# A two-layer decoder step: transposing a layer's outputs at the spill instead of at the load, and preparing a head's weights one head ahead

## The chip, the cores and the metric

The kernel runs on one NeuronCore of a Trainium2 chip. The metric is the time of one execution on the device, in microseconds (us). The core has a matrix engine (TensorE, PE in the profile, its weight loads PEld), three engines for elementwise work (VectorE = DVE, ScalarE = ACT, GpSimd = POOL), and SyncE (SP), which here only issues DMAs. Sixteen DMA engines move data between DRAM and the on-chip SBUF; matrix products land in PSUM. Each engine runs its own instructions in order and waits on semaphores for the others. So does SP: an issue that waits holds up every issue behind it.

## The reference

One inference step of a two-layer decoder, for a prompt of 2048 tokens and 8 samples of 4 tokens, with 1024 features:

```python
# layer 0: gated linear attention, 4 heads, key width 128, value width 512
proj = rmsnorm(h, norm_g) @ w_in              # q, k, v, gate, g_low
log_a = log_sigmoid(g_low @ w_gate2 + b_gate) / 16
o, state = gla_recurrence(q * 128**-0.5, k, v, log_a, state0)
h = h + (rmsnorm(o, out_norm_g) * silu(gate)) @ w_out
# keys and values shared by the next layer, from rmsnorm(h)
k, v = rope(rmsnorm(u @ w_k, k_norm)), u @ w_v
# layer 1: attention over a window of 128 positions, 32 query heads, 4 key heads
q, gate = split(rmsnorm(h, norm_g) @ w_in)
o = attend(rope(rmsnorm(q, q_norm_g)), k, v, sinks)
h = h + (o * silu(gate)) @ w_out
```

Inputs, weights and outputs are fp32. The outputs are both groups' results, the recurrent states of layer 0 and the last keys and values.

## The kernel before

**Numbers.** Each fp32 operand of a product is split into two fp16 halves, hi and lo, and the product is three fp16 matmuls (`PASSES`, L277). `split` (L184) makes the halves: ACT copies to fp16, and DVE or POOL subtracts. A weight is converted in steps of 128 x 512 elements (`Unit.convert`, L206): SP loads it raw into `wraw`, ACT scales and rounds it, DVE computes the remainder. Two ways lead from there:

- `load` (L229) converts straight into a buffer `W`, from which TensorE reads. There are 12 such buffers, each for 1024 columns, so for two steps.
- `prepare` (L234) converts into one of two `pst` buffers, and POOL issues a DMA that writes the halves to DRAM (`pre`, L242). Later `fetch` (L246) has SP load all of a unit into a `W`. Prepared steps are emitted with a lower priority (`behind`, L168).

**Layer 0** runs over 4 heads and, within a head, over 4 blocks (j = 0 to 3) of 512 tokens: 16 blocks (the loop at L926). A block computes q and k (48 matmuls of 512 columns), v and the gate for 4 chunks of 128 tokens (192), the block's scores by levels of halving with decays (`level_steps`, L487), and for each chunk the state update, the output and its norm (`chunk_steps`, L553). `weave` and `mix` (L145, L162) interleave lists of steps. Each block computes q, k and levels of the next one. The update of the states reads `ke`, the decayed keys, which SP transposes by DMA once per block (L545). In the first block of a head the 8 samples' states pass through (`sparts`), each by way of a `pst` buffer (L763).

At the end of a chunk `spill_og` (L607) splits its 128 x 512 outputs into halves in `ogT` (two buffers), ACT for hi and POOL for lo, and SP writes them to DRAM, `ogd[c]` (L610), tokens on the partitions.

The head's own weights come at two places. The q and k weights of the next head are loaded in its third block (L968 to L972). The v and gate weights are loaded and converted, 16 steps of `load`, in its last block: v at L953, when the old v weights are done with, the gate at L958.

The weights of layer 1 and combinations of its output weights are prepared in advance: a list `prep` of 144 steps (L866, L887), 8 rotary tables first, then 72 weight steps, then 64 steps for the combinations. `some(n)` (L868) takes the next n. In blocks from the third on, L966 takes `PR[j]` of them for each of three chunks, with `PR = (1, 4, 2, 0)`; so 3, 12, 6 and 0 a block, 63 in layer 0 in all. The last two blocks load the output weights of layer 0 instead.

**The output projection of layer 0** (`a_out`, L1034) runs over 16 chunks of 128 tokens, each 96 matmuls of 512 columns. `load` fetches a chunk's outputs with four transposing DMAs of 256 KB (L1041), so that features are on the partitions; it is called one chunk ahead (L1101, L1105). `fin` adds the residual, norms it and transposes the result by DMA into `uT` for layer 1. The first four chunks are woven into the end of layer 0's last block, with `few = 2` prepared steps in each of the chunks 1 to 3 (L1097 to L1102); the chunks 4 to 13 take `each = 7` (L1098, L1106), and the rest, 5, go to the end (L1491).

**Layer 1** runs 64 blocks in an order of TensorE that is written out (L1501), and then its output projection. Its own spill (`spill_halves`, L612) already transposes from SBUF to SBUF before it writes.

The order of instructions on each engine is otherwise made by a scheduler at build time, from the program's order, priorities and a simulated timeline.

Of the kernel before, what the change touches and what calls it, by code (L numbers as in the profile page):

```python
# [19 lines left out]
P = 128  # L20
# [32 lines left out]
SMC = 3  # L53
NV = 5
KL = 5
QL = 9
PR = (1, 4, 2, 0)

# [16 lines left out]
def _body(tc, nc, cp, sb, ps, dr, i, o):  # L75
# [12 lines left out]
    def C(tag, shape, dt):  # L88
        return cp.tile(shape, dt, tag=tag, name=tag)
# [28 lines left out]
    make_identity(nc, idh)  # L118
    mhalf = C("mhalf", [P, 16], F32)
    pool.memset(mhalf, -0.5)  # L120
# [16 lines left out]
    rtd = dr.tile([P, NCH, 4, HD], F32, tag="rtd", name="rtd")  # L137
    ogd = [dr.tile([P, 2, BW], F16, tag=f"ogd{c}", name=f"ogd{c}") for c in range(NCH)]
    ogd2 = [dr.tile([P, 2, 2, 8, P], F16, tag=f"oge{c}", name=f"oge{c}") for c in range(NCH)]
# [467 lines left out]
    def spill_og(og, dst, h, eng):  # L607
        ot = T("ogT", [P, 2, 512], F16, 2)
        split((ot[:, 0], ot[:, 1]), og, eng=eng)
        nc.sync.dma_start(dst[:, :, h * 512 : (h + 1) * 512], ot)  # L610

# [256 lines left out]
    def some(n=2):  # L868
        out = prep[:n]
        del prep[:n]  # L870
        return out
# [51 lines left out]
    samp = None  # L923
    sparts = []

    for n, (h, j) in enumerate(blocks):  # L926
# [7 lines left out]
        elif n == 1:  # L934
            side = u_steps(3) + [us_step]
        lv = nxt.level_steps() if nxt else []
        last = j == NBL - 1
        late = j == 0 and h > 0
# [11 lines left out]
        if last:  # L950
            ch = [cur.chunk_steps(c) for c in range(3)]
            weave([f for c in range(1, 4) for f in cur.vg_steps(c, (0,))], ch[0] + lv[:3] + ch[1][:3] + lv[3:5] + ch[2][:3])
            run(hw[h + 1].v.steps() if h + 1 < AH else wo.steps()[4:])  # L953
            for c in range(1, 4):
                weave(cur.vg_steps(c, (1,)), (ch[c - 1][3:] if c > 1 else []) + lv[3 + c * 2 : 5 + c * 2])
            for f in ch[2][3:]:
                f()
            run(hw[h + 1].g.steps() if h + 1 < AH else wo1.steps()[8:])  # L958
        else:
            for c in range(3):  # L960
                if n == len(blocks) - 2:
                    if c == 0:
                        wo_aside()
                    more = (wo1.steps()[:8] + wo.steps()[:4])[c * 4 : c * 4 + 4]
                else:
                    more = side[c * 2 : c * 2 + 2] if n < 2 else some(PR[j])  # L966
                weave(cur.vg_steps(c + 1, (0, 1) if n else (1,)), mix(cur.chunk_steps(c) + lv[(0,3,6)[c]:(3,6,8)[c]], sparts[(0,3,7)[c]:(3,7,99)[c]]) + more)
                if j == NBL - 2 and h + 1 < AH and c == 0:  # L968
                    hw[h + 1] = head_weights(h + 1)
                    for u in hw[h + 1].qk:  # L970
                        for f in u.steps():
                            f()  # L972
            sparts = []
# [60 lines left out]
    def a_out(c):  # L1034
# [3 lines left out]
        def load():  # L1038
            for q in range(4):
                ot.append(box_o["first"][:, q] if c == 0 else T(("sg", "v")[c % 2], [P, 8, P], F16, 4))  # L1040
                nc.sync.dma_start(ot[q], ogd[c][:, q % 2, q // 2 * D : q // 2 * D + D], transpose=True)  # L1041

# [52 lines left out]
    lead = 4  # L1095
    few = 2
    each = (len(prep) - 3 * few) // (tail - lead + 1) + 1  # L1097
# [207 lines left out]
    class SampleB:  # L1305
# [22 lines left out]
        def steps(self):  # L1328
# [141 lines left out]
            def att_3(tq):  # L1470
                Pc, VC, Vn = bx["Pc"], bx["VC"], bx["Vn"]
                pO = PT("kv", [P, GRP // 2, 4, TS])
                for b4 in range(4):
                    b = tq * 4 + b4
                    for pr in range(2):
# [4 lines left out]
                        for n, (a, z) in enumerate(PASSES):  # L1480
                            mm(out, Vn[:, z, :], rr(Pc[:, 1, a, b4]), start=False, stop=n == 2)
                of = T("skn2", [P, GRP // 2, 16], F32, 1)
                tk = slice(tq * 16, tq * 16 + 16)
# [342 lines left out]
```

## Time and profile before

| | us |
|---|---|
| median of 3 runs | 2831.7 |
| fastest, slowest | 2829.96, 2833.98 |
| the profiled execution | 2836.73 |
| its span, first to last instruction | 2834.9 |
| mean granted TensorE clock in it | 0.986 |

The stages of the profiled execution follow from the profile's matmuls: head 0 of layer 0 to about 345 us, heads 1 to 3 about 273 us each, the start of the output projection from about 1170, its steady part from 1245 to 1520, layer 1 to 2550 and its output projection to the end. A window's row in the profile gives the length of a stretch, the busy time of PE, PEld, DVE, ACT and POOL with their instruction counts, the granted TensorE clock as a share of full speed, the mean share of the DMA engines that were busy, and GB/s. A row of waits gives the total, the number of times and the longest. A row of a line gives count, shortest/median/longest duration in ns, and when the first and the last of them started. "SPq" is SP's issue of a DMA: its start and how long it took to issue. Matmuls are pipelined: one of 512 columns is shown with 379 ns, but 24 of them follow each other in 5.18 us.

### The profile page before, as it was taken

What the parts mean: (1) busy time and instruction counts of PE and PEld (TensorE: products, weight loads), DVE (VectorE), ACT (ScalarE), POOL (GpSimd) and SP (SyncE); (2) the same over time, 40 slices, a digit from 0 to 9 for tenths busy, and PEclk for the clock granted to TensorE, in tenths of its full rate; (3) what the DMA queues carried; (4) which work ended last, traced back from release to release, by engine and by line L of the source; (5) the groups of instructions that cost most, each with busy time, mean ns of one, the idle gap of its engine ahead of it and who ended that gap; (6) DMA issues with size and microseconds to landing.
All of it is one profiled execution on the core that took longest, in us unless ns stands there. A gap on an engine that the chain in (4) does not pass through costs nothing.

```text
span 2834.9 us, 51733 instructions
## 1 busy us (share of the span) xinstructions
PE 2716.0 (96%) x19258; PEld 1388.1 (49%) x19258; DVE 1699.3 (60%) x3470; ACT 1392.5 (49%) x3245; POOL 1145.7 (40%) x1600
## 2 busy tenths in 40 slices
PE   6899998999899999999899999999999999989999
PEld 4444544544454445444344555555555555544444
DVE  5665666566657655335422665677777777777653
ACT  6554655455546553433322555566666666651110
POOL 2352244224323421125503686566567567530000
PEclk9999999999999999999999999999999999999999
DMA  8351334134313533799987678978888899996431
GB/s 210 87 128 35 101 105 148 34 86 138 116 38 86 167 90 81 184 214 260 258 183 190 129 146 152 226 133 157 187 149 151 155 189 185 177 220 201 154 99 57
DMA packets 801029, 411.69 MB, mean 145 GB/s; under 512 B 644352, under 2 KB 717896, under 8 KB 800744
## 3 DMA queue, kind: packets, MB, share of 16 engines
q1 hardware_dynamic: 787816, 372.66, 57.5%
q0 software_dynamic: 10880, 35.66, 3.7%
q8 instruction: 150, 2.46, 0.4%
q14 instruction: 103, 0.84, 0.1%
q10 hardware_dynamic: 2080, 0.07, 0.0%
HBM read 161.97 MB, written 107.54 MB: 95 GB/s over the span
## 4 chain that ended last, share of the span: by engine, by line
PE 60%; DMA 9%; ACT 9%; DVE 8%; issue 6%; POOL 5%; SPq 1%; ACTq 0%; POOLq 0%; DVEq 0%
PE pj L101 35%; PE o L101 11%; PE tr L101 9%; PE kv L101 3%; ACT o L1261 2%; DVE v L192 2%; DMA pre<-pst 1%; PE lev L101 1%; ACT v L191 1%; DMA wraw<-in_a_w_in_dram 1%; DVE o L1256 1%; POOL ogT L189 1%; DMA pst<-v 1%; DMA uT<-ogT 1%; DVE lev L1256 1%
## 5 line engine op out<-in xcount | busy, mean ns | idle before, releaser
L101 PE MATMUL pj<-W,uT 128*128 128x512 f16 x5088 | 1198.8, 381 | 6.2 <-ACT sg L481 3.6
L101 PEld LDWEIGHTS <-uT 128*128 128x128 f16 x6976 | 650.5, 98 | 711.3 <-issue 36.7
L101 PE MATMUL tr<-W,uT 128*128 128x512 f16 x1536 | 365.6, 379 | 0.0
L180 POOL TENSOR_SCALAR rs_m<-ss 128x1 f32<-128x1 f32 (+3 forms) x186 | 40.0, 215 | 537.0 <-DVE ss L1158 186.2
L101 PEld LDWEIGHTS <-X 128*128 128x128 f16 x2744 | 185.1, 98 | 141.5 <-issue 15.8
L1261 ACT ACTIVATE o<-o,mx 128x256 f32<-128x256 f32 (+1 forms) x384 | 168.7, 439 | 165.9 <-DVE mx L1256 162.0
L101 PE MATMUL pj<-uT,W 128*128 128x512 f16 (+1 forms) x912 | 190.2, 358 | 26.1 <-DMA uT<-ogT 22.6
L1256 DVE CUSTOM_DVE_ANT_0 o<-o,madd,nsink 128x256 f32<-128x256 f32 (+1 forms) x384 | 183.8, 479 | 38.6 <-PE o L101 34.2
L192 DVE SCALAR_TENSOR_TENSOR v<-o,v 128x512 f16<-128x512 f32 (+1 forms) x192 | 129.0, 672 | 104.4 <-ACT v L191 102.2
L181 POOL TENSOR_TENSOR rs_r<-rs_m,mhalf 128x1 f32<-128x1 f32 (+3 forms) x182 | 185.0, 1016 | 13.4
L514 POOL TENSOR_TENSOR KQ<-KQ,bt 128x256 f32<-128x256 f32 x112 | 97.7, 873 | 229.1 <-DVE X L189 229.1
L101 PEld LDWEIGHTS <-W 128*128 128x128 f16 x2448 | 129.6, 99 | 114.2 <-issue 23.2
L101 PEld LDWEIGHTS <-v 128*128 128x128 f16 x976 | 95.3, 98 | 116.4 <-issue 4.4
L189 POOL TENSOR_TENSOR ogT<-og,ogT 128x512 f16<-128x512 f32 x68 | 82.2, 1208 | 123.8 <-ACT ogT L188 123.8
L101 PEld LDWEIGHTS <-sg 128*128 128x128 f16 x800 | 78.4, 99 | 106.3 <-DMA sg<-ogd 11.7
L188 ACT ACTIVATE X<-KQ 128x512 f16<-128x512 f32 x128 | 84.6, 661 | 74.2 <-PE lev L101 46.8
L101 PE MATMUL o<-gl,X 128*128 128x256 f16 (+1 forms) x768 | 113.9, 271 | 3.1 <-DMA X<-qe 1.7
L189 DVE TENSOR_TENSOR X<-KQ,X 128x512 f16<-128x512 f32 x128 | 98.5, 770 | 28.4 <-ACT X L188 27.4
L191 ACT ACTIVATE v<-o 128x512 f16<-128x512 f32 (+1 forms) x192 | 111.1, 579 | 3.6
L242 POOL DMA_DIRECT2D pre<-pst x72 | 50.4, 702 | 142.2 <-DVE pst L192 111.7
L1261 ACT ACTIVATE lev<-lev,mx 128x256 f32<-128x256 f32 (+1 forms) x128 | 56.5, 441 | 103.6 <-DVE mx L1256 101.5
L101 PE MATMUL pj<-W,v 128*128 128x512 f16 x448 | 104.4, 379 | 0.4 <-DMA v<-ogd 0.4
(437 smaller groups left out, 4848.0 us busy)
## 6 DMA issues: line engine op xcount, KB each, us to landing
pre<-pst POOLq DMA_DIRECT2D x72, 256.0 KB, 3.4
W<-pre SPq DMA_DIRECT2D x36, 512.0 KB
ogd<-ogT SPq DMA_DIRECT2D x68, 256.0 KB
wraw<-in_a_w_in_dram SPq DMA_DIRECT2D x64, 256.0 KB
wraw<-in_b_w_in_dram SPq DMA_DIRECT2D x64, 256.0 KB
oge<-og SPq DMA_DIRECT2D x64, 256.0 KB
wraw<-in_a_w_out_dram SPq DMA_DIRECT2D x32, 256.0 KB
X<-in_x_prompt_dram SPq DMA_DIRECT2D x32, 256.0 KB
```

Of the source, the lines that this page charges most:

```text
L101: return order(nc.tensor.matmul(*a, **k))
L180: pool.tensor_scalar(m[:n, :k], ss, a, b, ALU.mult, ALU.add)
L181: pool.tensor_tensor(r[:n, :k], m[:n, :k], mhalf[:n, :k], ALU.pow)
L188: act(hi, src, AF.Copy)
L189: eng.tensor_tensor(lo, src, hi, ALU.subtract)
L191: act(hi, src, AF.Copy, scale=sc)
L192: dve.scalar_tensor_tensor(lo, src, sc, hi, ALU.mult, ALU.subtract)
L242: nc.gpsimd.dma_start(self.pre[:, :, half * 512 : half * 512 + 512], t)
L514: pool.tensor_tensor(keys, keys, d[:, :, 1:2].to_broadcast([P, NB, m]), ALU.mult)
L1256: dve.tensor_tensor_reduce(pm[:, z], pm[:, z], madd.rearrange("p a b -> p (a b)")[:, (2 - nk) * P :], -0.125, nsink[:, g * GRP + h : g * G ...
L1261: act(pm[:, z], pm[:, z], AF.Exp, scale=-1.0, bias=nm_[:, h : h + 1], accum_out=bx["sum"][:, h : h + 1])
```

## The change

- `spill_og` transposes the two halves by a DMA from SBUF to SBUF into a new tile `ogk` (one buffer) and writes that to DRAM; `ogd` is laid out with features on the partitions. `a_out`'s load becomes a plain one of the same four pieces.
- The v and gate weights of heads 1 to 3 are no longer converted in the last block of the head before. They go through `prepare`: 16 steps, mixed with steps of `prep`. `steps()` of a prepared unit is `fetch`, so at L953 and L958 SP now loads 4 and 4 finished units.
- `PR` goes. A list `ahead` is filled at the second block of head 0 (16 steps and 2 of `prep`), at the first block of heads 1 and 2 (16 and 11), at the first block of head 3 (18 of `prep`) and at the last block of heads 0 to 2 (10 of `prep`). Each block takes 3 for each of three chunks; a last block takes 5 and then 2, 2 and 2. So layer 0 takes 72 steps of `prep` instead of 63, and it prepares 48 steps of its own weights that it converted in place before.
- `few` becomes 6, and `each` follows as 5.
- Two small tiles are cut or shared to make room in SBUF.

```diff
-PR = (1, 4, 2, 0)
+OGK = 1
-    ogd = [dr.tile([P, 2, BW], F16, tag=f"ogd{c}", name=f"ogd{c}") for c in range(NCH)]
+    ogd = [dr.tile([P, 2, BW // P, P], F16, tag=f"ogd{c}", name=f"ogd{c}") for c in range(NCH)]
...
     def spill_og(og, dst, h, eng):
         ot = T("ogT", [P, 2, 512], F16, 2)
         split((ot[:, 0], ot[:, 1]), og, eng=eng)
-        nc.sync.dma_start(dst[:, :, h * 512 : (h + 1) * 512], ot)
+        ok = T("ogk", [P, 2, 4, P], F16, OGK)
+        nc.sync.dma_start(ok.rearrange("p a k t -> p (a k) t"), ot.rearrange("p a x -> p (a x)"), transpose=True)
+        nc.sync.dma_start(dst[:, :, h * 4 : h * 4 + 4], ok)
...
+        if j == min(h, 1) ^ 1 and h + 1 < AH:
+            hw[h + 1] = head_weights(h + 1)
+            ahead = mix(hw[h + 1].v.prepare() + hw[h + 1].g.prepare(), some(11 if h else 2))
+        elif j == 0 and h > 0:
+            ahead = some(18)
+        elif j == NBL - 1 and nxt:
+            ahead = some(10)
+
+        def early(n):
+            out = ahead[:n]
+            del ahead[:n]
+            return out
...
-            weave([f for c in range(1, 4) for f in cur.vg_steps(c, (0,))], ch[0] + lv[:3] + ch[1][:3] + lv[3:5] + ch[2][:3])
+            weave([f for c in range(1, 4) for f in cur.vg_steps(c, (0,))], mix(ch[0] + lv[:3] + ch[1][:3] + lv[3:5] + ch[2][:3], early(5)))
...
-                weave(cur.vg_steps(c, (1,)), (ch[c - 1][3:] if c > 1 else []) + lv[3 + c * 2 : 5 + c * 2])
+                weave(cur.vg_steps(c, (1,)), mix((ch[c - 1][3:] if c > 1 else []) + lv[3 + c * 2 : 5 + c * 2], early(2)))
...
-                    more = side[c * 2 : c * 2 + 2] if n < 2 else some(PR[j])
+                    more = mix(early(3), side[c * 2 : c * 2 + 2])
...
                 if j == NBL - 2 and h + 1 < AH and c == 0:
-                    hw[h + 1] = head_weights(h + 1)
                     for u in hw[h + 1].qk:
...
-                nc.sync.dma_start(ot[q], ogd[c][:, q % 2, q // 2 * D : q // 2 * D + D], transpose=True)
+                nc.sync.dma_start(ot[q], ogd[c][:, q % 2, q // 2 * 8 : q // 2 * 8 + 8])
...
-    few = 2
+    few = 6
```

More of the change, by code (lines that the diff above doesn't have):

```diff
@@ L118, in _body @@
     make_identity(nc, idh)
-    mhalf = C("mhalf", [P, 16], F32)
+    mhalf = C("mhalf", [P, 8], F32)
     pool.memset(mhalf, -0.5)
@@ L924, in _body @@
     sparts = []
+    ahead = []
     for n, (h, j) in enumerate(blocks):
@@ L1481, in att_3 @@
                             mm(out, Vn[:, z, :], rr(Pc[:, 1, a, b4]), start=False, stop=n == 2)
-                of = T("skn2", [P, GRP // 2, 16], F32, 1)
+                of = T("skn", [P, GRP // 2, 16], F32, 2)
                 tk = slice(tq * 16, tq * 16 + 16)
```

## The prediction

> **What bounds the kernel now.** I read the page first, then the busy time by stages, then TensorE's idle time in slices of 10 us, then the waits behind the idle slices.
>
> ```profile
> span 2834.9 us, 51733 instructions
> PE 2716.0 (96%) x19258; PEld 1388.1 (49%) x19258; DVE 1699.3 (60%) x3470; ACT 1392.5 (49%) x3245; POOL 1145.7 (40%) x1600
> 550.00:823.00 273.00, 262.71 (x1733) 127.76 (x1732) 166.71 (x283) 149.03 (x262) 90.28 (x137) 0.99 0.32 97
> 1170.00:1245.00 75.00, 70.07 (x378) 31.82 (x377) 29.13 (x66) 26.72 (x52) 7.46 (x18) 0.95 0.78 181
> 1245.00:1520.00 275.00, 263.61 (x1430) 122.12 (x1430) 107.37 (x138) 76.75 (x149) 96.20 (x125) 0.98 0.94 235
> ```
>
> The columns of a stage are its length, the busy time of PE, PEld, DVE, ACT and POOL, the granted clock, the DMA share and GB/s. TensorE bounds the kernel: 2716.0 of 2834.9 us. So an edit can only win back idle time and the slow clock after it. The third row is one head of layer 0 (10.3 us idle, DMA at 0.32), the fourth the start of the output projection, the fifth its steady part (11.4 us idle, DMA at 0.94). The change takes DMA work from the full stage to the empty one, so these two places decide.
>
> ```profile
> 1360.00:1370.00 10.00, 10.00 (x48) 4.57 (x47) 7.52 (x7) 3.16 (x5) 8.49 (x10) 1.00 0.79 242
> 1370.00:1380.00 10.00, 4.54 (x22) 1.91 (x21) 7.04 (x8) 5.27 (x11) 7.80 (x11) 0.82 1.04 231
> 1380.00:1390.00 10.00, 7.90 (x26) 2.67 (x24) 3.28 (x5) 2.00 (x4) 2.42 (x5) 0.67 1.12 233
> 1390.00:1400.00 10.00, 7.72 (x29) 3.13 (x29) 5.39 (x5) 3.15 (x5) 4.13 (x5) 0.83 1.04 255
> 1379.86 1.04 PE L101 MATMUL pj<-W,sg 128*128 128x512 f16 x2 [5.46 <-DMA sg<-ogd]
> 1355.46 5.62 SPq L316 DMA_TRANSPOSE uT<-ogT  x2
> 1366.97 0.80 SPq L841 DMA_DIRECT2D KQ<-in_b_w_out_dram  x2
> 1371.72 7.42 SPq L1041 DMA_TRANSPOSE sg<-ogd  x3
> 1379.97 4.31 SPq L1041 DMA_TRANSPOSE sg<-ogd  x1
> ```
>
> This is nearly all that the output projection loses. A full slice holds 48 matmuls, these three hold 22 + 26 + 29 = 77 instead of 144: 67 x 10/48 = 14.0 us lost, 9.8 as idle and the rest as clock (0.67). TensorE waits for the spilled outputs of the next chunk: SP issues their four transposing loads at 1371.72 to 1384, and the DMA engines are full.
>
> ```profile
> 277.00:345.00 68.00, 68.00 (x551) 34.95 (x548) 42.38 (x69) 39.85 (x74) 17.36 (x29) 1.00 0.31 92
> 345.00:412.00 67.00, 66.36 (x462) 33.39 (x460) 44.93 (x91) 41.08 (x72) 24.21 (x38) 1.00 0.31 93
> 412.00:480.00 68.00, 59.74 (x324) 27.12 (x322) 46.76 (x75) 43.61 (x73) 34.63 (x46) 0.97 0.58 182
> 480.00:550.00 70.00, 70.00 (x427) 33.53 (x426) 31.71 (x51) 24.01 (x44) 18.27 (x30) 1.00 0.10 27
> 685.00:754.00 69.00, 61.72 (x346) 28.97 (x345) 47.56 (x74) 39.92 (x70) 35.32 (x46) 1.00 0.57 180
> 958.00:1028.00 70.00, 62.03 (x336) 28.35 (x334) 46.79 (x73) 47.84 (x76) 33.83 (x45) 0.98 0.51 162
> PE kv L101 <- ACT v L191: 11.8, 9, 1.8
> ```
>
> The first four rows are four blocks in turn: the last of head 0 and the first three of head 1. The idle time of a head lies in one of them: 8.3 us in the third row, 7.3 in its like of the next head, 8.0 in that of the third, 23.6 in all. The last row (waits of PE from 277 to 1097) names the largest cause: the state update waits for v, which ACT splits late. These rows hold the conversions of later weights:
>
> ```profile
> L191 ACT ACTIVATE pst<-wraw,gsb x64: 705/721/723, 433.3 to 1281.7; 128x512 f16<-128x512 f32 x64
> L192 DVE SCALAR_TENSOR_TENSOR pst<-wraw,gsb,pst x64: 733/751/1653, 434.0 to 1282.4; 128x512 f16<-128x512 f32 x64
> L242 POOL DMA_DIRECT2D pre<-pst x72: 668/691/789, 406.0 to 1285.2; - x72
> ```
>
> PR deals 3, 12, 6 and 0 steps to the blocks of a head, and the chip runs most of the 18 of the middle two in the third row, 0.72 us of ACT, 0.75 of DVE and 0.69 of POOL each.
>
> **The change, part by part.** All sums are against the profiled execution: 2836.73 us, 1.8 of it outside the span. The median of the three runs, 2831.7, is 5.0 lower, and I apply the difference to the median.
>
> *Plain loads in the output projection: -13 us.* The price of a transposing load comes from two windows, 1440 to 1500 us and 1492 to 1499 us:
>
> ```profile
> q1 hardware_dynamic: 19400, 13.25, 86.6%
> v<-ogd SPq DMA_TRANSPOSE x8
> sg<-ogd SPq DMA_TRANSPOSE x4
> uT<-ogT SPq DMA_TRANSPOSE x2
> q1 hardware_dynamic: 876, 2.84, 102.4%
> ```
>
> The second window has plain transfers only: 2.84 MB in 7 us, so 256 KB keep all 16 engines busy for 0.65 us. In the first, 14 transposes of 256 KB are 3.67 of 13.25 MB; the other 9.58 MB cost 23.6 us at that rate, and the busy time is 0.866 x 60 = 52.0, which leaves 28.4 us or 2.0 us for each transpose. A chunk of 20.7 us (96 matmuls) thus sheds 4 x (2.0 - 0.65) = 5.4 us of DMA, and 0.94 becomes about 0.68. SP also sheds time, since it took over 10 us to issue four. If the loads are again issued at 1371.7, they land within about 3 us, and TensorE needs them at 1374.4. Bounds 0 and -14; I take -13. The next in line there is the transpose of the normed rows, whose reader comes four chunks later.
>
> *The start of the output projection: -3 us.*
> ```profile
> 1220.00:1230.00 10.00, 7.53 (x42) 3.18 (x40) 2.62 (x6) 2.16 (x4) 0.20 (x1) 0.98 0.92 210
> 1230.00:1240.00 10.00, 9.35 (x38) 3.63 (x37) 3.18 (x7) 2.99 (x7) 0.73 (x1) 0.68 0.54 172
> 1228.88 0.18 PE L101 MATMUL o<-qe,pst 128*128 128x8 f16 x1 [2.38 <-ACT pst L191]
> ACT pst L191 <- DMA bt<-in_state_gla_dram: 23.3, 5, 7.7
> ```
>
> TensorE loses 3.1 us as idle here and some 2 us as clock (0.68): the sample states come late through the same full DMA engines, and that is eased. Against it, six conversions instead of two in each of three chunks (few) pass through the same two pst buffers as the states. Bounds -5, and +9 if 12 more conversions of 0.72 us on ACT each hold a state up.
>
> *Even dealing of conversions: -12 us.* The sum of conversions in the first three blocks of heads 1 and 2 goes from 21 to 27; 16 leave the last block, where now 10 run. DVE over the three blocks of head 1 is (44.93 + 46.76 + 31.71)/205 = 60%; six more add 4.5 us: 62%. The first row above shows a block at 42.38/68 = 62% DVE with 16 conversions, those of the next head's weights, and no idle time at all. So truly even dealing would take back the 23.6 us. But an engine runs a conversion as soon as its buffers allow, so clumps stay; and the first block of a head, which has the sample states, goes from 3 to 9 conversions: (44.93 + 4.5)/67 = 74% DVE. Bounds 0 and -24; the first row speaks for the whole, the 74% for nothing, and I take half.
>
> *The head's weights through DRAM: 0.* In the last block 16 conversions become 8 fetches of 512 KB. The same 4 MB are read at the same place; removed are two operations on the way. TensorE's wait at a head's turn is for v, 1.76 us at the second (the last row of the fence on SP below). 48 spills of 256 KB and their fetches, 25 MB, at the rate above are 62 us of DMA, with 68 transposes of 2.0 us 198 us over 1170: 0.32 becomes about 0.5, which leaves room. On POOL 57 more issues of 0.69 us are 39 us over heads in which it is busy for 90.28 of 273 us. Bounds -5 and +5, one such wait more or less at three turns.
>
> *Head 0: +2 us.* Its second and third blocks get nine conversions each beside the norms of x. The second:
>
> ```profile
> 150.00:210.00 60.00, 54.74 (x303) 25.34 (x301) 36.23 (x65) 35.99 (x72) 34.29 (x49) 0.97 0.58 139
> ```
>
> DVE goes from 60% to 72%, and 5.3 us are idle already. Bounds 0 and +7, the DVE time of nine.
>
> *The transpose at the spill: +2 us.* POOL's subtract frees SP as before; then SP issues a transpose, waits until it lands, and issues the write:
>
> ```profile
> L610 SPq DMA_DIRECT2D ogd<-ogT x68: 533/545/1439, 106.6 to 1156.4; - x68
> L617 SPq DMA_TRANSPOSE og<-ogT x64: 1231/1268/3751, 1584.3 to 2565.0; - x64
> SPq L618 <- DMA og<-ogT: 56.8, 51, 3.8
> SPq L610 <- POOL ogT L189: 344.6, 54, 22.3
> 614.22 1.37 SPq L545 DMA_TRANSPOSE ke<-X  x1
> 623.66 0.38 PE L101 MATMUL kv<-v,ke 128*128 128x512 f16 x1 [1.76 <-ACT v L191]
> ```
>
> The same sequence runs in layer 1: 1.27 us to issue and 1.1 us more of waiting (56.8/51). With the write 0.55 us, SP is held about 2.4 us longer at each of 68 spills (64, and one repeated in each head's last block). Behind it wait raw weights, fetches, sample states and one transpose of ke per block. SP already stands 344.6 us at this place without TensorE waiting for it. ke is issued 9.4 us before its first reader. Bounds 0 and +39 (below).
>
> Sum: -13 - 3 - 12 + 0 + 2 + 2 = -24. Median: 2831.7 - 24 = **2807.7, say 2807**.
>
> **The rivals.** *The clumps move.* Sample states, nine conversions and level steps meet in the first block, and as much is lost there as is won in the second: even dealing counts 0, the rest -12: 2820. For it speaks that the third row's clump is made by eager engines, not by PR alone; against it the first row.
>
> *SP becomes the wait* (slower). Two spills stand ahead of ke in SP's order, each 2.4 us longer, and its landing slips behind the first state update. That uses the 9.4 us of lead less some 3 to land. If one spill per block then shows in full, 16 x 2.4 = 39 us: 2831.7 - 24 + 39 = 2847. It decides once SP reaches ke about 6 us later than now. Against it: no wait of TensorE for ke is in the trace.
>
> *The transposes are not what fills the output projection.* From 1361.1 to 1367.0 SP issued nothing and then a conversion's load, before the first of the four at 1371.7; if that order alone made the gap, plain loads issued as late would leave it, and the two terms of that stage go: 2831.7 - 24 + 16 = 2824. The Trainium skill has a rule of this kind: Advanced Engine Details and Errata, X-Bar Transpose (TRN2), says that transposing DMAs are as fast as regular ones. By that rule the loads would shed no DMA time. The trace disagrees, with 2.0 against 0.65 us for 256 KB.
>
> *All comes back.* The upper bounds of both main terms: -14 - 24 - 5 + 2 + 2 = -39: 2793.
>
> **How the numbers follow.** Forecast 0.60, with its own range 2797 to 2819; clumps move 0.15; SP 0.12; transposes innocent 0.05; all back 0.08. The range leaves out the SP rival and the far end of the last case: 2787 to 2834. About 0.2% (6 us) is what a measurement of this kernel can tell from no change: faster is below 2826, slower above 2837. The clumps and transposes cases reach into that band with their bounds, so same gets 0.08, slower 0.13, faster 0.79.
>
> **What would show it.** Right: no wait of PE on the output projection's loads, DMA there near 0.7, its stage shorter by about 14 us; conversions spread over the head's blocks, with less than 12 us idle in the three blocks together; 68 transposes in layer 0 with DMA near 0.5. Wrong: PE waiting for ke, W or pst; idle time of 5 us or more in the first block of a head; layer 1 (from 1520) changed by more than 5 us, which nothing here explains.

## The result, and the profile after

The changed kernel takes **2872.43 us** (median of 5 runs, 2870.78 to 2876.62) beside 2833.1 for the kernel before in the same comparison: a ratio of 1.0144 (95% interval 1.0129 to 1.0159). It is slower by 1.4%, where 1% faster was forecast, and far outside the range.

The page of the changed kernel, its span, busy times and the first row of its chain by lines:

```profile
span 2870.2 us, 52007 instructions
PE 2721.4 (95%) x19258; PEld 1390.9 (48%) x19258; DVE 1708.6 (60%) x3470; ACT 1388.2 (48%) x3243; POOL 1183.0 (41%) x1648
PE pj L101 32%; PE o L101 11%; PE tr L101 9%; DMA pre<-pst 4%; PE kv L101 3%; ACT o L1276 2%; DMA pst<-v 2%; DVE v L192 1%; ACT v L191 1%; PE lev L101 1%; DVE pst L192 1%; POOL ogT L189 1%; DVE o L1271 1%; POOL rs_r L181 1%; DVE lev L1271 1%
```

TensorE and DVE execute the same number of instructions as before and are busy 5 and 9 us more; POOL has 48 more issues and is busy 37 us more. In the chain that ended last, the write of a converted weight (`pre<-pst`) now holds 4%. The same row of the kernel before:

```profile
PE pj L101 35%; PE o L101 11%; PE tr L101 9%; PE kv L101 3%; ACT o L1261 2%; DVE v L192 2%; DMA pre<-pst 1%; PE lev L101 1%; ACT v L191 1%; DMA wraw<-in_a_w_in_dram 1%; DVE o L1256 1%; POOL ogT L189 1%; DMA pst<-v 1%; DMA uT<-ogT 1%; DVE lev L1256 1%
```

To see where the 35.3 us of span came from, I cut both traces at the same matmuls: the first sample projection of each head (it stands at the start of the head's last block), the first and the last `o<-uT,v` product of the output projection, the first of the samples' last products (`lev<-ogTs,uT`), which stand at the end of layer 1. So "head 1" below runs from the last block of head 0 to the last block of head 1.

Each time is of one execution, the profiled one.

| stage | before | changed | difference | forecast |
|---|---|---|---|---|
| to the last block of head 0 | 282.6 | 307.1 | **+24.5** | +2 |
| head 1 | 272.1 | 279.7 | +7.6 | heads 1 to 3 together: -12 |
| head 2 | 273.2 | 281.6 | +8.4 | |
| head 3 | 273.0 | 272.1 | -0.9 | |
| to the first product of the output projection | 75.8 | 74.7 | -1.1 | these two: -16 |
| output projection | 332.2 | 324.0 | -8.2 | |
| layer 1 | 1036.5 | 1042.5 | +6.0 | 0 |
| the end | 289.5 | 288.5 | -1.0 | 0 |

Busy times by stages of the changed kernel (the columns as before; the last three rows stand beside the three stages shown in the prediction):

```profile
60.00:307.00 247.00, 209.42 (x1207) 98.26 (x1206) 147.49 (x242) 129.73 (x234) 107.10 (x163) 0.92 0.60 138
587.00:868.00 281.00, 266.06 (x1732) 128.56 (x1729) 167.83 (x284) 153.16 (x269) 106.96 (x161) 0.98 0.50 140
1208.50:1283.50 75.00, 64.36 (x337) 28.81 (x336) 34.43 (x66) 27.35 (x53) 16.93 (x26) 0.93 0.67 195
1283.50:1558.50 275.00, 274.71 (x1513) 129.33 (x1511) 98.69 (x130) 69.44 (x141) 87.07 (x116) 1.00 0.72 220
```

and of the kernel before in head 0:

```profile
60.00:282.60 222.60, 203.34 (x1214) 96.88 (x1212) 131.44 (x223) 117.50 (x216) 89.48 (x137) 0.95 0.38 88
```

The steady part of the output projection did what was forecast: 0.3 us idle instead of 11.4, clock 1.00 instead of 0.98, DMA at 0.72 (forecast 0.68). Five conversions a chunk instead of seven have a part in that; e1 below keeps the seven. Head 0 is the surprise: 37.6 us idle (247 - 209.42) instead of 19.3, and the clock down from 0.95 to 0.92 with it. In head 2 TensorE idles 14.9 us where it idled 10.3, at 0.98 instead of 0.99. The start of the output projection, too, idles 10.6 us instead of 4.9.

Three of the larger rows of TensorE's waits in the whole changed kernel (total, times, longest; the largest, 22.0 us for `uT`, was 22.6 before):

```profile
PE pj L101 <- ACT sg L481: 14.4, 5, 4.9
PE kv L101 <- ACT v L191: 10.8, 9, 1.9
PE pj L101 <- ACT KQ L438: 8.3, 3, 3.3
```

The waits that the prediction had named as signs of failure stay small in layer 0 and its output projection: 6.7 us in 12 waits for `pst`, none over 1.2, 0.3 for `ke`, no row for `W`. What grew are waits for products of ACT that were late: `sg`, the Silu of the gate, had 3.6 us before, and `KQ` are the q and k rows; `v` is as before (11.8). Of the other signs, the first blocks of heads 1 and 2 idle only 1.3 and 2.1 us, but layer 1 changed by more than 5 us, and heads 1 and 2 idle 15.7 and 14.9 us, where less than 12 was the sign of being right. The next view shows a stop in the making: the order of time in head 0 of the changed kernel, 259 to 279 us (start, duration, engine and operation, idle time before it and what released it):

```profile
259.46 1.27 SPq L611 DMA_TRANSPOSE ogk<-ogT  x1
265.12 0.57 SPq L612 DMA_DIRECT2D ogd<-ogk  x1
265.79 1.06 SPq L880 DMA_DIRECT2D pst<-in_c_rope_dram  x2
...
268.90 0.71 POOL L885 TENSOR_TENSOR pst<-pst,gq 128x256 f32<-128x256 f32 x1 [4.98 <-DMA pst<-in_c_rope_dram]
...
270.27 0.18 POOL L180 TENSOR_SCALAR rs_m<-ss 128x1 f32<-128x1 f32 x1
270.42 0.66 POOL L514 TENSOR_TENSOR KQ<-KQ,bt 128x256 f32<-128x256 f32 x1
...
271.11 0.63 ACT L188 ACTIVATE X<-KQ 128x512 f16<-128x512 f32 x1 [7.42 <-POOL KQ L514]
271.99 0.59 POOL L181 TENSOR_TENSOR rs_r<-rs_m,mhalf 128x1 f32<-128x1 f32 x1
...
272.61 0.75 DVE L601 SCALAR_TENSOR_TENSOR og<-o,rs_r,sg 128x512 f32<-128x512 f32 x1 [8.32 <-POOL rs_r L181]
...
274.05 0.80 PE L101 MATMUL lev<-X 128*128 128x64 f16 x12 [4.87 <-ACT ogT L188]
```

One step of preparation, here a rotary table, stands on POOL and waits 4.98 us for its load. Behind it in POOL's order wait the decayed `KQ`, which ACT needs (7.42 us idle), and the norm's `rs_r`, which DVE needs (8.32 us idle). All three engines stop for a piece of work that nobody needs before layer 1, and TensorE then stops for 4.87 us. The load itself is late because of the other part of the change. SP issues the transpose of a spill at 259.46 and stands 4.3 us until it has landed (265.12); the table's load is next in SP's order. The other long stop of head 0 (TensorE 4.94 us, to 187.28) has the same order: transpose at 175.18, its write at 180.91, a table's load at 181.63, for which POOL waits 5.86 us. At a weight step POOL waits in another place, before it issues the write, for DVE's lower half. The waits of POOL and ACT at such steps in head 1, 307 to 587 us of the changed kernel:

```profile
POOL pre L242 <- DVE pst L192: 41.8, 23, 4.6
ACT pst L191 <- DMA pre<-pst: 23.5, 12, 3.8
```

and in the kernel before, 282 to 555 us:

```profile
POOL pre L242 <- DVE pst L192: 16.0, 7, 4.1
ACT pst L191 <- DMA pre<-pst: 7.2, 5, 2.7
```

### The profile page after: what moved, and what is told of

It is laid out like the page before. It is cut to its first block, busy times and chain, and to the rows that moved or that the text cites. A ratio compares the mean times of both kernels' runs of the same rounds, so it can differ in the third digit from the quotient of the medians.

```text
span 2870.2 us, 52007 instructions
## 1 busy us (share of the span) xinstructions
PE 2721.4 (95%) x19258; PEld 1390.9 (48%) x19258; DVE 1708.6 (60%) x3470; ACT 1388.2 (48%) x3243; POOL 1183.0 (41%) x1648
## 4 chain that ended last, share of the span: by engine, by line
PE 57%; DMA 12%; ACT 9%; issue 8%; DVE 8%; POOL 6%; SPq 1%; POOLq 0%; ACTq 0%; DVEq 0%
PE pj L101 32%; PE o L101 11%; PE tr L101 9%; DMA pre<-pst 4%; PE kv L101 3%; ACT o L1276 2%; DMA pst<-v 2%; DVE v L192 1%; ACT v L191 1%; PE lev L101 1%; DVE pst L192 1%; POOL ogT L189 1%; DVE o L1271 1%; POOL rs_r L181 1%; DVE lev L1271 1%
## 5 line engine op out<-in xcount | busy, mean ns | idle before, releaser
L101 PE MATMUL pj<-W,uT 128*128 128x512 f16 x5088 | 1209.0, 382 | 24.5 <-ACT sg L481 14.4
L242 POOL DMA_DIRECT2D pre<-pst x120 | 83.8, 701 | 190.7 <-DVE pst L192 154.4
L189 DVE TENSOR_TENSOR qe<-KQ,qe 128x512 f16<-128x512 f32 x80 | 85.3, 1066 | 36.5 <-ACT qe L188 35.7
```

Of the source, the lines that this page charges most:

```text
L101: return order(nc.tensor.matmul(*a, **k))
L189: eng.tensor_tensor(lo, src, hi, ALU.subtract)
L242: nc.gpsimd.dma_start(self.pre[:, :, half * 512 : half * 512 + 512], t)
```

## The experiments

Two theories stood against each other. **P**: what costs is preparation, the steps that pass through a `pst` buffer and are written to DRAM, because they put in-order waits on ACT, DVE and POOL. **S**: what costs is SP, which now waits at 68 transposes (the slower rival of the prediction). The first four kernels separate the change's parts.

**The spill alone** (e1_spill_only): the kernel before with the diff's `spill_og`, `ogd` and plain load; `PR`, `few` and the in-place weights as before, the two small tiles as in the change.

```diff
-        nc.sync.dma_start(dst[:, :, h * 512 : (h + 1) * 512], ot)
+        ok = T("ogk", [P, 2, 4, P], F16, OGK)
+        nc.sync.dma_start(ok.rearrange("p a k t -> p (a k) t"), ot.rearrange("p a x -> p (a x)"), transpose=True)
+        nc.sync.dma_start(dst[:, :, h * 4 : h * 4 + 4], ok)
```

> The kernel before with the transpose at the spill and the plain load only; conversions are dealt as before. Theory P (the loss comes from sending the heads' own weights through pst, POOL's DMA and DRAM, which puts waits on the in-order ACT, DVE and POOL): no loss in layer 0, and the output projection wins 8 to 14 us, so 2819 to 2826 us beside 2833 of before. Theory S (SP, held by each transpose until it lands, delays layer 0): layer 0 loses its 32 to 40 us here too, so 2855 to 2866.

Measured: 2824.53, ratio 0.9973 (0.9961 to 0.9985). This is P's range, and S falls as a cause by itself. Head 0 is 2.9 us longer, heads 1 to 3 together 0.3 shorter, the output projection 10.3 shorter.

**The preparation alone** (e2_ahead_only): the changed kernel with the old spill, layout and load.

```diff
-        ok = T("ogk", [P, 2, 4, P], F16, OGK)
-        nc.sync.dma_start(ok.rearrange("p a k t -> p (a k) t"), ot.rearrange("p a x -> p (a x)"), transpose=True)
-        nc.sync.dma_start(dst[:, :, h * 4 : h * 4 + 4], ok)
+        nc.sync.dma_start(dst[:, :, h * 512 : (h + 1) * 512], ot)
```

> The changed kernel with the spill and the load as before, so the weights ahead and the new dealing alone. Theory P: layer 0 loses as much as in the changed kernel, and the output projection's gap is back: 2874 to 2886 us. Theory S: layer 0 is as before, 2828 to 2842.

Measured: 2860.09, ratio 1.011 (1.0088 to 1.0132). Neither range holds: 18 us above S, and 14 below P. Alone, the parts are worth -8 and +27 us; together they give +39. Some 20 us come only from both; more on this below.

**Head 0 as before** (e4_head0_as_before): the changed kernel, but head 1's own weights are converted in place in the last block of head 0, and head 0 takes six steps of `prep`.

```diff
-        if j == min(h, 1) ^ 1 and h + 1 < AH:
+        if h == 0:
+            ahead = some(6) if j == 2 else []
+        elif j == 0 and h + 1 < AH:
```

> The changed kernel, but in head 0 the weights of head 1 are converted in place in its last block as before, and only 6 steps of prep run in its third block. Theory P: the 24 us that head 0 lost (sample projection of head 0 at 307 us instead of 283) are gone, the 8 us each of heads 1 and 2 stay: 2844 to 2852 us. Theory S: the transposes at the spill are all there, so at most a few us change: 2865 to 2873.

Measured: 2850.76, ratio 1.0069 (1.0046 to 1.0092). Head 0 is back at 282.9 us with all its transposes: P's range holds, and the whole +24.5 hangs on the steps put there.

**The rotary tables later** (e5_rotary_later): in the list `prep` the eight tables stand behind the 72 weight steps, since the wait in the timeline above is at a table.

```diff
-    prep = [lambda n=n, w=w, hf=hf: rope_table(n, w, hf) for n in range(2) for w in range(2) for hf in range(2)] + prep
+    prep_w = prep
+    prep = [lambda n=n, w=w, hf=hf: rope_table(n, w, hf) for n in range(2) for w in range(2) for hf in range(2)]
+    prep = prep_w[:72] + prep + prep_w[72:]
```

> The changed kernel with the 8 rotary tables behind the 72 weight steps of prep, so out of head 0. Theory R (in head 0 POOL stands in order for a rotary table's load, with the level products and rsqrt behind it): the idle piece of 4.9 us at 274 us and its like near 185 us go, with their slow clock, 8 to 15 us: 2857 to 2864. Theory P without R: weight steps that take the tables' places cost as much, 2868 to 2876.

Measured: 2865.21, ratio 1.012 (1.0101 to 1.0139), between the two, 7.2 us below the changed kernel. In the profiled execution, the slowest of the four (2872.41), head 0 wins 2.9 us and head 1 loses 7.4. Weight steps stand where the tables stood, and POOL waits for them as well: its waits for DVE ahead of the writes in head 0 go from 30.4 to 41.0 us. So the tables are at most a small part of it.

The next ones ask what about a step costs: the ring of buffers, the dealing, the number, or the detour by DRAM.

**A third buffer** (e6_third_pst): e2 with three `pst` buffers instead of two at all their uses; the one in `prepare`:

```diff
-                t = T("pst", [P, 2, 512], F16, 2)
+                t = T("pst", [P, 2, 512], F16, 3)
```

> e2 (weights ahead, spill and load as before) with a third pst buffer everywhere. Theory P1 (ACT stands in order before a conversion until an earlier spill from the same pst buffer has landed, with work that TensorE needs queued behind it; the loss grows with the number of pst steps in a stretch): ACT's waits for pre<-pst in heads 0 to 2 fall to below half (21.5 us in head 1 of e2), and heads 0 to 2 win 5 to 15 us of the 27 lost, 2845 to 2855 beside 2860 of e2. Theory P2 (the fetch of the finished units from DRAM, or its traffic, is what costs): nothing changes in layer 0, 2857 to 2863.

Measured: 2863.27, ratio 1.0102 (1.0075 to 1.0128): no gain over e2. ACT's wait for a buffer in heads 1 and 2 (293 to 853 us) with three buffers,

```profile
ACT pst L191 <- DMA pre<-pst: 39.0, 30, 4.1
```

and with two (297 to 855 us):

```profile
ACT pst L191 <- DMA pre<-pst: 38.2, 21, 3.5
```

A third buffer did not shorten these waits, so having only two is not what costs here. Head 0 is 3.8 us shorter than in e2, head 3 7.0 longer; what does set the waits was not tried.

**Even dealing alone** (e7_even_in_place): e1 with one line changed.

```diff
-PR = (1, 4, 2, 0)
+PR = (2, 2, 3, 0)
```

> e1 (spill alone) with PR = (2, 2, 3, 0), so 6, 6 and 9 steps in the first three blocks instead of 3, 12 and 6; the heads' weights are converted in place as before. If dealing evenly is worth what the prediction said, heads 1 to 3 win 4 us each: 2810 to 2816 beside 2824.5 of e1. If the clumps only move: 2821 to 2828.

Measured: **2817.9**, ratio 0.9949 (0.9928 to 0.9969), the fastest kernel of the study, faster than the kernel before and the changed one. Against e1, head 2 is 6.5 us shorter, head 3 2.9, head 1 not at all. Head 2 of e7, where TensorE now idles 7.5 us at full clock (lines in the kernels built on e1 stand one later than in the kernel before):

```profile
556.00:824.00 268.00, 260.47 (x1734) 127.65 (x1733) 166.82 (x284) 153.56 (x269) 95.07 (x145) 1.00 0.42 116
```

**More steps, weights in place** (e9_same_number_in_place): e1 with nine steps of `prep` in each of the first three blocks of heads 1 and 2 (27 instead of 21 a head).

```diff
-                    more = side[c * 2 : c * 2 + 2] if n < 2 else some(PR[j])
+                    more = side[c * 2 : c * 2 + 2] if n < 2 else some(3 if h in (1, 2) else PR[j])
```

> e1 with 9, 9 and 9 pst steps in heads 1 and 2, as many as the changed kernel has there, but all of them of prep; the heads' own weights are converted in place in the last block as before. Theory P1: heads 1 and 2 lose what they lost in the changed kernel, 5 to 10 us each (270.5 and 274.5 us from one sample projection to the next in e1), so 2832 to 2842 less what 12 steps fewer in the output projection save (0 to 4 us). Theory P2: both heads as in e1 within 3 us, 2819 to 2827.

Measured: 2830.3, ratio 0.9992 (0.9979 to 1.0005), above P2's range and at the lower edge of P1's, 2832 to 2842 less the 2.4 us that the output projection saved. Head 1 is at 278.7 us, close to the changed kernel's 279.7, without any weight going by DRAM that did not before; head 2 hardly moves (275.1 after 274.5). So twelve more steps cost 8.8 us, but not evenly, and the count of steps does not tell where.

**Weights ahead, but no more steps** (e10_ahead_not_more): e1 where the 16 own steps of heads 2 and 3 go through `pst` in place of as many steps of `prep`, so that 21 a head remain. The steps of `prep` that were pushed out go to the output projection, 10 a chunk instead of 7.

```diff
+        if j == 0 and h in (1, 2):
+            hw[h + 1] = head_weights(h + 1)
+            ahead = mix(hw[h + 1].v.prepare() + hw[h + 1].g.prepare(), some(5))
...
-                    more = side[c * 2 : c * 2 + 2] if n < 2 else some(PR[j])
+                    more = side[c * 2 : c * 2 + 2] if n < 2 else [ahead.pop(0) for _ in range((2, 2, 3)[j])] if h in (1, 2) else some(PR[j])
```

> e1 with the weights of heads 2 and 3 ahead, in place of steps of prep, so that the first three blocks of heads 1 and 2 keep 21 pst steps, dealt 6, 6 and 9; their last blocks have 8 fetches and no conversion. The 32 steps of prep go to the output projection (10 a chunk instead of 7). Theory P1: heads 1 and 2 as in e1 or better, 535 to 546 us together (545.0 in e1). Theory P2: 5 to 8 us more each, 555 to 561. The output projection (321.9 us in e1) gains 0 to 15 us in length by its three more conversions a chunk; 2815 to 2840 in all by P1, 2835 to 2856 by P2.

Measured: 2866.02, ratio 1.011 (1.0077 to 1.0143). Heads 1 and 2 take 547.5 us, 2.5 more than in e1, 8.8 more than in e7 with the same dealing: the detour itself costs 1 to 4 us a head. From there to the changed kernel, with 32 steps more in the two heads, it is another 13.8 us. Neither range holds for the whole kernel, because the output projection went from 321.9 to 354.0 us, where at most 15 more were expected. Its steady part, and what TensorE and ACT wait for in it (three views of e10):

```profile
1247.00:1530.00 283.00, 254.28 (x1352) 115.44 (x1351) 128.41 (x161) 92.92 (x172) 116.92 (x155) 0.95 0.88 277
```

```profile
PE pj L102 <- DMA v<-ogd: 15.9, 4, 8.2
PE pj L102 <- DMA sg<-ogd: 10.9, 6, 5.7
```

```profile
ACT pst L192 <- DMA pre<-pst: 60.0, 27, 5.3
```

TensorE again waits for the chunks' loads, although they are plain: ten conversions a chunk bring the DMA share back to 0.88, and ACT stands 60 us at its ring. So the output projection has little room either; with seven a chunk (e1) one such wait, of 5.5 us, was left.

The last four ask for the size and the mechanism.

**Eighteen steps in head 0** (e11_head0_prep): e7 with 16 weight steps of `prep` and two tables in the second and third blocks, 0 and 9 before.

```diff
+        if n == 1:
+            ahead = mix(prep[8:24], prep[:2])
+            del prep[8:24]
+            del prep[:2]
...
-                    more = side[c * 2 : c * 2 + 2] if n < 2 else some(PR[j])
+                    more = mix(ahead[:3], side[c * 2 : c * 2 + 2]) if n < 3 else some(PR[j])
+                    del ahead[:3]
```

> The kernel with the transposed spill and PR = (2, 2, 3, 0), all heads' own weights converted in place, but with 9 prepared steps in each of the second and third blocks of head 0 (16 weight steps and 2 rotary tables, mixed in as the changed kernel mixes them) instead of 0 and 9 (8 rotary tables and a weight). Head 0 takes 285.5 us without this and 307.1 in the changed kernel. Theory N (prepared steps cost whatever weight they hold: POOL and ACT wait in order for each other and for the write): head 0 at 297 to 306 us, whole kernel 2829 to 2838. Theory O (the cost is that of the next head's own weights, fetched in the last block, with ten more steps there): head 0 at 285 to 291 us, whole kernel 2816 to 2823.

Measured: 2825.95, ratio 0.9981 (0.9965 to 0.9996). Head 0 takes 294.2 us, 8.7 more than in e7: between the two ranges, so neither theory holds in full.

**Without the ten of the last block** (e14_no_ten): the changed kernel, where the last block of head 0 adds nothing to `ahead`.

```diff
-        elif j == NBL - 1 and nxt:
+        elif j == NBL - 1 and nxt and h > 0:
```

> The changed kernel without the ten prepared steps in the last block of head 0 (they follow in the output projection, whose share goes from 5 to 6 a chunk). Head 0 takes 307.1 us in the changed kernel and 294.2 in the one with 18 prepared steps of other weights in its second and third blocks, ten fewer in its last, own weights in place. Theory T (the other 13 us are those ten steps, in a block that TensorE fills without idle time in the kernel before): head 0 at 292 to 298 us, whole kernel 2858 to 2865. Theory F (they are the price of holding the head's own weights ahead and fetching them, or of the spill's transposes beside them): head 0 at 303 to 308 us, whole kernel 2868 to 2876. The start of the output projection, heads 1 to 3 and layer 1 stay within 4 us of the changed kernel by both.

Measured: 2856.95, ratio 1.0086 (1.0069 to 1.0103). Head 0 takes 298.6 us instead of 307.1: 8.5 of the 13 us go, which is just above T's range and 4 us under F's, and the whole kernel is 1 us below T's. In the profiled execution head 1 (3.9 us) and the output projection (3.8) are shorter, too. The ten steps stand in the program's last block of the head, but the time is lost ahead of it, because all ten run there, earlier than the program has them. Four groups of the changed kernel (60 to 307 us; a row of counts and times each) show all 8 tables and 4 more weight steps before 307 us, beside the 16 of the own weights:

```profile
L191 ACT ACTIVATE pst<-wraw,gsa x16: 705/722/722, 153.8 to 236.0; 128x512 f16<-128x512 f32 x16
L880 SPq DMA_DIRECT2D pst<-in_c_rope_dram x8: 327/360/563, 181.6 to 266.5; - x8
L887 POOL DMA_DIRECT2D rtd<-pst x8: 926/938/978, 187.7 to 274.2; - x8
L191 ACT ACTIVATE pst<-wraw,gskv x4: 721/722/722, 274.5 to 286.2; 128x512 f16<-128x512 f32 x4
```

**SP issues the writes** (e12_sp_writes): the changed kernel with one word changed in `prepare`.

```diff
-                nc.gpsimd.dma_start(self.pre[:, :, half * 512 : half * 512 + 512], t)
+                nc.sync.dma_start(self.pre[:, :, half * 512 : half * 512 + 512], t)
```

> The changed kernel with one difference: SP, not POOL, issues the DMA that writes a converted weight from pst to DRAM. Theory Q (POOL's in-order issue is the cost: while POOL waits for DVE's lower half before it can issue the write, its KQ products, rsqrt and lower halves of the outputs are queued behind, and ACT and DVE wait for those): head 0 falls from 307.1 to 285-293 us, heads 1 and 2 from 279.7 and 281.6 to 270-275, whole kernel 2822 to 2845. Theory B (the cost is the ring of two pst buffers, that is the time until the write has landed, or the plain work of the conversions): head 0 stays above 300, heads 1 and 2 above 277, whole kernel 2865 to 2880. Against Q stands only that SP in its turn waits for DVE in order, with raw weights behind.

Measured: 2855.6, ratio 1.0093 (1.0072 to 1.0114), 17 us below the changed kernel, and in neither range. Head 0 falls to 299.3 us and head 2 to 275.4, head 1 stays (280.6). So POOL's place in the order is part of it, some 17 of the 39 us, but not all; in heads 1 and 2 it is 5.3 of 16.0. The group of these issues in the changed kernel (120 of them, 0.70 us each; after the bar the idle time before them):

```profile
L242 POOL DMA_DIRECT2D pre<-pst x120 | 83.8, 701 | 190.7 <-DVE pst L192 154.4 <-DVE ss L302 22.4 <-DVE k L795 5.6
```

The issues themselves are 83.8 us; the waits ahead of them are 190.7, and what stands behind them on POOL is held up too. The Trainium skill (Trainium Kernel Development and Optimization, Key Constraints) says that DMAs of all issuing queues run on the same 16 engines, and that issuing from several only saves issue time. Here the choice of the queue also decides who else stands in line behind the wait.

**SP issues the writes, on e7** (e13_even_sp): the same one word as in e12.

> The kernel with the transposed spill and PR = (2, 2, 3, 0), own weights in place (2817.9 us), with SP instead of POOL issuing the writes of prepared weights. Theory Q (POOL's in-order issue): 2806 to 2814 us, heads 1 to 3 at 265-268 us instead of 270.7, 268.0 and 270.1. Theory B (ring or plain work): 2816 to 2822, or above that where SP's waits hold raw weights up in the output projection.

Measured: 2819.11, ratio 0.9961 (0.9947 to 0.9975), no difference from e7's 2817.9. That would fit a POOL with slack enough for its waits at 21 steps a head and not at 37; no run between the two was made.

The stages of all kernels side by side, with the number of steps that passed through `pst` in them (tables included, counted by the issues of their writes in the trace):

| kernel | steps to the last block of head 0 | us | steps in heads 1 and 2 | us |
|---|---|---|---|---|
| before | 6 | 282.6 | 42 | 545.3 |
| e1, spill alone | 6 | 285.5 | 42 | 545.0 |
| e7, and even dealing | 9 | 285.5 | 42 | 538.7 |
| e13, e7 with writes by SP | 9 | 285.5 | 42 | 542.5 |
| e10, weights ahead, not more | 6 | 284.1 | 42 | 547.5 |
| e11, 18 in head 0 | 18 | 294.2 | 42 | 544.0 |
| e9, more steps | 6 | 285.5 | 54 | 553.8 |
| e14, without the ten | 18 | 298.6 | 74 | 556.5 |
| e4, head 0 as before | 6 | 282.9 | 74 | 560.6 |
| e12, writes by SP | 28 | 299.3 | 74 | 556.0 |
| e2, old spill | 28 | 297.0 | 74 | 557.7 |
| e5, tables later | 28 | 304.2 | 74 | 567.5 |
| e6, old spill, third buffer | 28 | 293.2 | 74 | 559.8 |
| changed | 28 | 307.1 | 74 | 561.3 |

More steps go with more time in both columns: 24.5 us for 22 more steps in head 0, 16.0 for 32 more in heads 1 and 2 (22.6 against e7, which deals them evenly too), so 0.5 to 1.1 us of TensorE's time for each on average. It is not a fixed price. With the same 28 steps head 0 takes 293.2 to 307.1 us, and with the same 74 heads 1 and 2 take 556.0 to 567.5; the spill, the issuing engine and the dealing (6 of 545 us from e1 to e7) each move a stage. How far one such time repeats is known only in part: e1, e7, e9 and e13 agree on 285.5 us in head 0.

## Why the prediction was wrong

**Plain loads, -13: right in the main.** The steady part of the output projection lost all its idle time. Alone (e1) the stage won 10.3 us, since one wait for a load stayed; in the changed kernel, with 5 conversions a chunk instead of 7, none did, but its start took back some of the gain (next term), so the stage won 8.2. That the transposes fill the DMA engines shows in the shares: 0.94 at 235 GB/s before, 0.80 at 245 in e1 with the same seven conversions; per byte the engines are busy 18% less. So the rival by which transposes are innocent does not hold as a whole. The Trainium skill's rule quoted there (X-Bar Transpose (TRN2) of Advanced Engine Details and Errata) does not hold in this kernel either, by the same shares. But the rival was right that SP's order makes a wait of its own. In e1 SP issues the four plain loads only after two transposes of normed rows, when TensorE has just run out of work (the first row is the steady part of e1):

```profile
1246.70:1521.70 275.00, 268.16 (x1463) 125.08 (x1462) 109.18 (x140) 75.82 (x149) 102.19 (x136) 0.99 0.80 245
1390.96 4.13 SPq L317 DMA_TRANSPOSE uT<-ogT  x2
1395.19 2.51 SPq L1044 DMA_DIRECT2D v<-ogd  x4
1400.53 12.04 PE L102 MATMUL pj<-W,v 128*128 128x512 f16 x48 [5.46 <-DMA v<-ogd]
```

**Start of the output projection, -3: wrong sign, inside its bounds.** In the counterpart of that window TensorE idles 10.6 us, 5.7 more than before. The bound of +9 had named the cause, `few` = 6 beside the sample states: TensorE waits once 5.2 us for a product of ACT that the samples need (`ssm`), and twice for `pst`. With `few` = 2 (e1) the same window idles 2.9 us, 2.0 less than before, as forecast. Two rows of TensorE's waits in the changed kernel, 1208 to 1560 us:

```profile
PE lev L101 <- ACT ssm L188: 5.2, 1, 5.2
PE o L101 <- ACT pst L191: 1.3, 2, 0.8
```

No run changes `few` alone, but the kernels bear it out: the wait for `ssm` is there, 2.7 to 7.5 us, in e2, e4, e6, e12 and e14, all with `few` = 6, and in none of e1, e7, e9, e10, e11 and e13 with `few` = 2. In e5, also with 6, it is absent; there eight of these steps are tables, in which ACT has no part.

**Even dealing, -12: right in direction by itself, and outweighed.** Alone (e7 against e1, whose head 3 also takes three steps fewer) it won 9.2 us in heads 1 to 3 and 6.6 on the median. The step that failed is the premise beside it: the prediction's first block row, full at 62% DVE with 16 conversions, was taken as proof that a block bears conversions. Those were conversions *in place*. They end in a `W` buffer that TensorE reads, with no write behind them, and taking all 16 out of the last blocks of heads 1 and 2, in exchange for the detour, won nothing (e10). A conversion through `pst` is another thing: ACT waits until an earlier write has landed, POOL waits for DVE, and the block's own work queues behind both (the timeline and the waits above). Busy shares did not show this; the changed kernel's DVE is at 60% in head 2 (167.83/281), no more than forecast.

**The head's weights through DRAM, 0 (-5 to +5): the main error.** The working counted DMA time and 57 issues of 0.69 us on POOL, against slack in both. The DMA share came out as forecast (0.50), and the detour in exchange for other steps costs 1 to 4 us a head (e10). But it was no exchange: 16 steps a head that had been harmless became 16 more of the costly kind, 37 instead of 21. The waits ahead of POOL's issues, 16.0 us in head 1 before, were in the trace and were not multiplied. With them at 41.8 us, and ACT's at the ring up from 7.2 to 23.5, heads 1 and 2 lost 16 us where even dealing had been booked as a gain. Taking the issues off POOL wins back 5 of the 16 (e12); how the rest divides over ACT, DVE and SP no run shows.

**Head 0, +2 (0 to +7): too small by a factor of ten.** The working counted 18 steps by DVE's time alone, with the measure for in-place conversions again. Of the +24.5, up to 2.9 are the spill's (e1; in e4, with the same spill, head 0 shows none of it), some 9 follow from the 18 steps in place of 9 (e11) and 8.5 from the ten that were written for the last block but moved forward (e14); the prediction left those at the last block, where they would have been hidden. The other 4 are not told apart, and the parts do not simply add: beside the preparation the spill is worth 10.1 us in head 0 (e2 to the changed kernel).

**Transpose at the spill, +2: right by itself** (e1: 2.6 us over the heads), too small beside the preparation. The sum looked only for a wait for `ke`; what SP's stop delays in head 0 are loads for the steps behind it. In head 1 SP waits longer for the landing than forecast, 2.1 us (35.1/17) instead of 1.1. SP's row in head 1 of the changed kernel:

```profile
SPq L612 <- DMA ogk<-ogT: 35.1, 17, 3.7
```

**Left open.** The 20 us that appear only with both parts. Going from e2 to the changed kernel, the spill adds 10.1 us to head 0 and 2.6 to head 1, where it added 2.9 and took 1.6 off by itself; it takes 5.0 instead of 10.3 off the output projection, and layer 1 is 5.3 longer instead of 1.4 shorter. Part of the first is in the traces: the two long stops of head 0 begin behind SP's waits for the landing, which there last 31.4 us in all and up to 4.5 (25.4 and 3.0 in e1), and in e2, without them, TensorE has no stop of that length. But taking the tables away (e5) won only 2.9 us in head 0, and no run frees SP from these waits with the preparation in place. Layer 1, +6, took 1035 to 1045 us in the kernels of this study with no edit to it but a shared tile; in the changed kernel TensorE waits 12.5 us instead of 7.6 there for one transposing load (`pst<-v`). What moves it was not tried.

## What to carry to other kernels

In this kernel a step of side work cost by what its engines wait for in order more than by how long they are busy: before moving one into a buffer ring with a write behind it, count the waits at the steps already there and multiply those. Work that is converted straight into its final place can be free in a block where the same work through a ring is not, so a profile without idle time says only that the present kind is borne. And a change of several parts is worth taking apart, and its parts worth pricing together: two waits that are harmless alone can stand in line. Transposed spill and even dealing with the weights left in place (e7) give 0.9949 of the time before, where all of it together gives 1.0144.

## What the runs showed that was not expected

- A buffer more in a ring did not shorten the waits at it (38.2 us in 21 waits with two buffers, 39.0 in 30 with three).
- Moving the issue of 120 writes from POOL to SP won 17 us in the changed kernel and nothing in e7, where 72 go over and a head has 21 steps.
- A short stop can cost twice, though not each does: the slice from 530 to 540 us of the changed kernel idles 4.4 us at a granted clock of 1.00. The slice with the stop of the timeline above has 20 matmuls instead of 48 or more and a granted clock of 0.64, the next one 0.84 (start, length, busy time of PE, PEld, DVE, ACT and POOL, clock, DMA share, GB/s):

```profile
270.00:280.00 10.00, 3.92 (x20) 1.73 (x20) 7.09 (x10) 3.66 (x6) 7.92 (x12) 0.64 0.29 70
280.00:290.00 10.00, 10.00 (x58) 4.43 (x56) 6.45 (x9) 4.66 (x9) 4.68 (x8) 0.84 0.96 206
```
